# Nine of twelve modulation vectors: from fp32 matmuls and VectorE sums to ScalarE products with GpSimd sums

## Chip, cores and metric

The kernel runs on one core of a Trainium2 chip. The metric is the time of one execution on the device in microseconds (us). Engines are called as the profile calls them: PE (TensorE), ACT (ScalarE), DVE (VectorE), POOL (GpSimd), SP (SyncE, which issues the transfers here).

## What is computed

Two layers of a transformer trunk over 128 context tokens and 128 latent tokens, all in float32, model width D = 2048. Of the reference this matters here:

```
def trunk_layer(x, cond, lp, rope, ctx_k, ctx_v, s0):
    ...
    m = jax.nn.silu(cond) @ w_ada + b_ada
    ...
    sh1, sc1, g1, sh2, sc2, g2 = jnp.split(m, 6, axis=-1)
    h = x * (1.0 + sc1) + sh1
    mix, k, v, s_fin = mixer(h, ...)
    x = layer_norm(DN_ALPHA * x + g1 * mix, ln1_g, ln1_b)
    h = x * (1.0 + sc2) + sh2
    gate, up = jnp.split(h @ w_gate_up, 2, axis=-1)
    ffn = (jax.nn.silu(gate) * up) @ w_down
    x = layer_norm(DN_ALPHA * x + g2 * ffn, ln2_g, ln2_b)
```

The modulation m is one row of 6 x 2048 per stream (context and latent) and layer, made from a 2048 x 12288 matrix w_ada per layer, 201 MB for both. The six vectors of a layer have the numbers 0 to 5 (sh1, sc1, g1, sh2, sc2, g2). The mixer holds the input product (w_in), eight gated DeltaNet heads, attention and the output product (w_o).

## The kernel before

**The large products.** Every weight is read once, 1 MB at a time (`wtile`), into one of two buffers `r`. ACT copies each half as a high part H in fp32r (L382, the "cast"), DVE makes the low part L = r - H (L383). There are three buffers of H and L. PE then multiplies high by high, low by high and high by low: `col_mm` (L413, L414, L417) with the weight as stationary operand, `row_mm` (L390, L391, L393) with the activations as stationary operand. In the feed-forward part of a layer the hidden width is cut in three (HALVES); each third runs w_gate_up tiles, then w_down.

**What runs between.** Both product loops call a hook after every quarter of a tile. In the mixer the hook (`weave`) advances generators of the DeltaNet heads and of attention, and `fill`; in the feed-forward part it is `fill` alone. `fill(n)` adds n to a debt and takes one step of the modulation queue per whole unit, RATES giving n by layer and stage.

**The modulation.** Vectors 0 and 1 of layer 0 are needed first and come from `ada_part`. The other ten stand in `order` and come from `ada_vec`: a vector is 32 tiles of 128 x 1024 of w_ada (one step and one SP load of 512 KB each). On PE a tile is four fp32 matmuls (L253) with the 32 columns of `scT`, which holds silu(cond), as stationary operand; they stand side by side in the array. In the feed-forward part a share of the tiles (DVE_PART) goes to DVE instead: L250 adds tile times scalar to four running sums `side`, the first tile of a run being copied by ACT (L248), and `side_sum` brings them together over the partitions with a matmul of ones (L218). Then the bias is added, and the vector goes to columns (`mods`) or to DRAM (`grow`).

**Who needs a vector when.** `ensure(l, vec)` runs the queue until a vector is done. It stands ahead of the residual with g1, ahead of `fold` for the next layer norm, and ahead of the feed-forward residual with g2; for layer 0 that is right after the first third, since LATE[0] is False. `tail` ends each half of a layer; GAP steps of the queue stand between its two streams.

**The scheduling.** The program hands all this to a scheduler that keeps program order but for priorities (`ahead`, PRI). Each engine then runs its own queue in order. SP issues the weight loads, and each waits for its buffer. POOL has little to do: the memsets, `rsq` (L150, L151), and for each DeltaNet unit an affine_select (L767). L704 and L708 are DVE steps of the DeltaNet heads with two SBUF inputs, L763 one with an input in PSUM.

Of the kernel before, what the change touches and what calls it, by code (L numbers as in the profile page):

```python
# [9 lines left out]
F32 = mybir.dt.float32  # L10
# [25 lines left out]
GAP = (2, 2)  # L36
# [4 lines left out]
LATE = (False, True)  # L41
YLD = (0, 1, 2)
DVE_PART = (0.7, 1.0)
# [3 lines left out]
RATES = ((4.4, 2.0, 1.2), (0.55, 0.6, 0.4))  # L47
# [36 lines left out]
def trunk(ctx: ExitStack, tc: tile.TileContext, A: dict, O: dict):  # L84
# [12 lines left out]
    adap = pool("ada", 1)  # L97
# [6 lines left out]
    def ahead(i):  # L104
        return tc.high_priority(offset=PRI[i]) if PRI[i] else nullcontext()
# [13 lines left out]
    # ------------------------------------------------------------------ constants  # L119
    crow = cp.tile([32, 128], F32, name="crow")  # L120
# [12 lines left out]
    ctan = cp.tile([32, 128], F32, name="ctan")  # L133
# [19 lines left out]
    # ------------------------------------------------------------------ modulation  # L153
# [5 lines left out]
    def ada_part(l, vec, k0, nk, wide=False):  # L159
        """Modulation columns of nk channel tiles (2 or 4) from k0 on."""  # L160
# [20 lines left out]
        br = adap.tile([128, 512], F32, tag="br", name="br")[:, 0:256]  # L181
# [20 lines left out]
    side = {"alloc": None, "ring": None, "part": 0.0, "due": 0.0, "open": None}  # L202

    def side_start(alloc, ring, part):
        side.update(alloc=alloc, ring=ring, part=part, due=0.0)

    def side_stop():
        side.update(alloc=None, ring=None)
        if side["open"] is not None:
            side_sum(False)  # L210

    def side_sum(stop):
        """Add the vector engine's partial products of the open half to the sums of the tensor engine."""
        ps, h, a = side["open"]
        side["open"] = None
        for v in range(2):
            for q in range(4):
                nc.tensor.matmul(ps[32 * q:32 * q + 32, h * 256:(h + 1) * 256], lhsT=ones[:, v, :],  # L218
                                 rhs=a[v][q // 2][:, q % 2 * 256:q % 2 * 256 + 256], start=False,
                                 stop=(stop and v == 1), tile_position=(0, 32 * q))  # L220

    def ada_vec(l, vec):
        ps = psD.tile([128, 512], F32, tag="ada", name="psv")
        started = False
        for h in range(2):
            for kt in range(KT):
                c0 = vec * D + h * 1024
                end = h == 1 and kt == KT - 1
                use = False
                if side["alloc"] is not None:  # L230
                    side["due"] += side["part"]
                    use = side["due"] >= 1.0 and started
                if use and side["ring"] is not None:
                    r = side["ring"]()
                else:
                    r = rawp.tile([128, 1024], F32, tag="a", bufs=RAW[1], name="ra")
                nc.sync.dma_start(r, A["w_ada"][l, kt * 128:(kt + 1) * 128, c0:c0 + 1024])
                if use:
                    side["due"] -= 1.0
                    first = side["open"] is None  # L240
                    if first:
                        side["open"] = (ps, h, side["alloc"]())
                    for v in range(2):
                        for c in range(2):
                            av = side["open"][2][v][c]
                            rc = r[:, c * 512:(c + 1) * 512]
                            if first:
                                nc.scalar.activation(av, rc, AF.Copy, scale=scT[:, kt, v:v + 1])  # L248
                            else:
                                nc.vector.scalar_tensor_tensor(av, rc, scT[:, kt, v:v + 1], av, ALU.mult, ALU.add)  # L250
                else:
                    for q in range(4):
                        nc.tensor.matmul(ps[32 * q:32 * q + 32, h * 256:(h + 1) * 256], lhsT=scT[:, kt, :],  # L253
                                         rhs=r[:, q * 256:(q + 1) * 256], start=not started,
                                         stop=(end and side["open"] is None), tile_position=(0, 32 * q))
                    started = True
                if kt == KT - 1 and side["open"] is not None:
                    side_sum(end)
                if not end:
                    yield  # L260
        br = adap.tile([128, 512], F32, tag="br", name="br")
# [20 lines left out]
    order = [(0, 2), (0, 4), (0, 3), (0, 5)] + [(1, v) for v in (1, 0, 2, 4, 3, 5)]  # L282
# [22 lines left out]
    def ensure(l, vec):  # L305
        while (l, vec) in state["q"] or (state["gen"] is not None and state["cur"] == (l, vec)):
# [6 lines left out]
    # ------------------------------------------------------------------ parameter columns  # L313
# [48 lines left out]
    # ------------------------------------------------------------------ weight tiles and products  # L362
    def wtile(src, nk, n, src2=None, store=None):
# [9 lines left out]
        for j in range(nk // 2):  # L373
# [7 lines left out]
            with ahead(3 if side["alloc"] is None else 4):  # L381
# [42 lines left out]
    class Act:  # L424
        """Transposed activations [channel, channel tile, stream, token] as a high and a low part."""
# [903 lines left out]
```

## Time and profile before

| what | value |
|---|---|
| three runs | 2826.47, 2827.35 (median), 2832.9 us |
| the profiled execution: span from first to last instruction | 2828.9 us; the record has no time outside it |
| instructions | 49217 |
| mean granted PE clock | 0.990 of full speed |
| HBM read / written | 642.88 MB / 8.98 MB, 230 GB/s over the span |

The busy time of an engine is the union of its instructions. An instruction that is held up while it runs counts as busy for all of it. Matmul ends are modelled and overlap, and POOL spans are rough. The idle time in front of a group is put down to what ended it. The stages used below are windows in us from the span's start.

### The profile page before, as it was taken

How to read it: one execution, taken by the hardware profiler on the slowest of the kernel's cores; microseconds unless marked ns; L12 is line 12 of the kernel's file. 1: busy time of each engine (PE TensorE's matmuls, PEld its weight loads, DVE VectorE, ACT ScalarE, POOL GpSimd, SP SyncE). 2: the span in 40 equal slices, each digit the busy share in tenths (PEclk: the TensorE clock that was granted, in tenths of full speed). 3: DMA queues.
4: the chain of work that ended last, by engine and by line, in shares of the span. 5: the costliest groups of instructions: out<-in, count | busy, mean ns of one | idle time of the engine just before them, and what ended most of it. 6: DMA issues, size and time to landing. Idle time of an engine off the chain costs nothing.

```text
span 2828.9 us, 49217 instructions
## 1 busy us (share of the span) xinstructions
PE 2716.8 (96%) x19577; PEld 2321.9 (82%) x19577; DVE 1984.6 (70%) x3008; ACT 1272.6 (45%) x2186; POOL 77.4 (3%) x223
## 2 busy tenths in 40 slices
PE   7999999999999999999999999999899999999998
PEld 5778766667998799878987998877699889998996
DVE  2666877858987878777787587776865855555456
ACT  3324656534444334434435466664444344443442
POOL 0000001000000000000000000100000000000000
PEclk9999999999999999999999999999999999999999
DMA  7888876578888888788876644447766755656555
GB/s 254 262 264 302 260 229 211 175 268 274 271 292 282 299 277 282 262 285 275 277 253 225 227 156 130 156 132 236 254 194 199 250 206 184 211 187 208 184 182 186
DMA packets 406968, 655.08 MB, mean 232 GB/s; under 512 B 19648, under 2 KB 244178, under 8 KB 406610
## 3 DMA queue, kind: packets, MB, share of 16 engines
q1 hardware_dynamic: 406738, 651.94, 70.0%
q8 instruction: 153, 2.51, 0.4%
q14 instruction: 77, 0.63, 0.1%
HBM read 642.88 MB, written 8.98 MB: 230 GB/s over the span
## 4 chain that ended last, share of the span: by engine, by line
PE 47%; DMA 11%; DVE 10%; issue 3%; ACT 3%; POOL 1%; SPq 0%; DVEq 0%; ACTq 0%; POOLq 0%
PE acc L413 10%; PE acc L414 10%; PE acc L417 10%; PE acc L390 4%; PE acc L391 4%; PE acc L393 4%; DMA sa<-w_ada 4%; DVE L L383 4%; DVE side L250 4%; DMA r<-w_down 3%; DMA r<-w_gate_up 3%; ACT H L382 1%; DMA r<-w_o 1%; PE psv L253 1%; PE pr L826 1%
## 5 line engine op out<-in xcount | busy, mean ns | idle before, releaser
L382 ACT ACTIVATE H<-r 128x1024 fp32r<-128x1024 f32 (+1 forms) x770 | 796.1, 1041 | 1202.1 <-PE acc L414 396.0
L383 DVE TENSOR_TENSOR L<-r,H 128x1024 fp32r<-128x1024 f32 (+1 forms) x770 | 922.2, 1201 | 566.5 <-ACT H L382 560.3
L413 PE MATMUL acc<-h2H,H 128*128 128x256 f32 x2816 | 741.6, 285 | 10.3 <-DVE fth L1233 7.8
L414 PE MATMUL acc<-h2L,H 128*128 128x256 f32 x2816 | 736.9, 283 | 0.2 <-DVE h2L L477 0.2
L417 PE MATMUL acc<-h2H,L 128*128 128x256 f32 x2816 | 568.6, 283 | 1.1 <-DVE L L383 0.9
L413 PEld LDWEIGHTS acc<-h2H,H 128*128 128x128 f32 x2816 | 540.6, 192 | 27.4 <-issue 11.9
L414 PEld LDWEIGHTS acc<-h2L,H 128*128 128x128 f32 x2816 | 541.0, 192 | 1.0 <-DVE hf L471 0.4
L417 PEld LDWEIGHTS acc<-h2H,L 128*128 128x128 f32 x2816 | 439.5, 192 | 2.5 <-DVE L L383 2.2
L250 DVE SCALAR_TENSOR_TENSOR side<-sa,scT,side 128x512 f32<-128x512 f32 x480 | 339.1, 745 | 45.4 <-DMA sa<-w_ada 45.0
L390 PE MATMUL acc<-H,dH 128*128 128x512 f32 x672 | 268.9, 400 | 8.7 <-DVE fth L1233 6.0
L391 PE MATMUL acc<-H,dL 128*128 128x512 f32 x672 | 266.2, 396 | 0.0
L413 PE MATMUL acc<-hH,H 128*128 128x256 f32 x768 | 210.1, 295 | 4.3 <-ACT H L382 4.1
L393 PE MATMUL acc<-L,dH 128*128 128x512 f32 x672 | 212.0, 396 | 0.3 <-DVE L L383 0.2
L414 PE MATMUL acc<-hL,H 128*128 128x256 f32 x768 | 203.7, 286 | 0.0
L390 PEld LDWEIGHTS acc<-H,dH 128*128 128x128 f32 x672 | 126.6, 188 | 48.3 <-DVE fth L1233 7.7
L413 PEld LDWEIGHTS acc<-hH,H 128*128 128x128 f32 x768 | 147.8, 192 | 17.7 <-issue 9.1
L417 PE MATMUL acc<-hH,L 128*128 128x256 f32 x768 | 157.7, 288 | 0.1
L390 PE MATMUL acc<-H,hH 128*128 128x392 f32 (+1 forms) x384 | 153.5, 400 | 4.3 <-ACT H L382 4.3
L393 PEld LDWEIGHTS acc<-L,dH 128*128 128x128 f32 x672 | 126.3, 188 | 31.6 <-DVE L L383 1.2
L253 PE MATMUL psv<-ra,scT 128*32 128x256 f32 x1504 | 133.2, 396 | 19.1 <-DMA ra<-w_ada 19.0
L391 PEld LDWEIGHTS acc<-H,dL 128*128 128x128 f32 x672 | 126.6, 188 | 29.4
L414 PEld LDWEIGHTS acc<-hL,H 128*128 128x128 f32 x768 | 148.1, 193 | 1.8 <-issue 1.6
(286 smaller groups left out, 3392.5 us busy)
## 6 DMA issues: line engine op xcount, KB each, us to landing
r<-w_gate_up SPq DMA_DIRECT2D x352, 512.0 KB
ra<-w_ada SPq DMA_DIRECT2D x244, 512.0 KB
r<-w_down SPq DMA_DIRECT2D x88, 1024.0 KB
sa<-w_ada SPq DMA_DIRECT2D x132, 512.0 KB
r<-w_in SPq DMA_DIRECT2D x48, 1024.0 KB
r<-w_o SPq DMA_DIRECT2D x32, 1024.0 KB
r<-w_in SPq DMA_DIRECT2D x24, 784.0 KB
r<-w_in SPq DMA_DIRECT2D x32, 512.0 KB
```

Of the source, the lines that this page charges most:

```text
L250: nc.vector.scalar_tensor_tensor(av, rc, scT[:, kt, v:v + 1], av, ALU.mult, ALU.add)
L253: nc.tensor.matmul(ps[32 * q:32 * q + 32, h * 256:(h + 1) * 256], lhsT=scT[:, kt, :], rhs=r[:, q * 256:(q + 1) * 256], start=not started, ...
L382: nc.scalar.activation(H[:, :w], rs_, AF.Copy)
L383: nc.vector.tensor_tensor(L[:, :w], rs_, H[:, :w], ALU.subtract)
L390: nc.tensor.matmul(a[:, :n], lhsT=act.stat(0, kt, s), rhs=H[:, i, :], start=(first and i == 0), stop=False)
L391: nc.tensor.matmul(a[:, :n], lhsT=act.stat(1, kt, s), rhs=H[:, i, :], start=False, stop=False)
L393: nc.tensor.matmul(a[:, :n], lhsT=act.stat(0, kt, s), rhs=L[:, i, :], start=False, stop=(last and i == 1))
L413: nc.tensor.matmul(a, lhsT=H[:, i, cs], rhs=xH, start=(f and i == 0 and b % 2 == 0), stop=False)
L414: nc.tensor.matmul(a, lhsT=H[:, i, cs], rhs=xL, start=False, stop=False)
L417: nc.tensor.matmul(a, lhsT=L[:, i, cs], rhs=xH, start=False, stop=(la and i == 1 and b % 2 == 1))
L826: nc.tensor.matmul(p[:, d * 128:(d + 1) * 128], lhsT=X[:, d, 0], rhs=v[:, d], start=True, stop=True)
```

## The change

One vector of layer 0, (0, 4), stays with `ada_vec`, now on PE alone. The nine others, (0, 2), (0, 3), (0, 5) and all of layer 1, come from `pool_all`. A vector is four parts of 512 columns. Each step of a part loads two channel tiles (one load of 512 KB), multiplies each by the scalar of each of the two streams on ACT (four 128x512 products, L253 in the new file) and adds them to the two running sums `pacc` on POOL (L256). The products of stream 0 go to a scratch tile `pp` with one buffer, those of stream 1 overwrite the weight tile `pw`, which has two. Three steps into the next part, `pool_finish` sums `pacc` over the partitions with eight matmuls of ones (L264). Steps come from `pfill` in the same hooks, at the rates of POOL_RATES. Besides, LATE[0] becomes True (the gated residual of layer 0 is formed once, in its last third, from rows stored in DRAM), GAP becomes 0, and small buffers move to make room.

```
-GAP = (2, 2)
+GAP = (0, 0)
+PLAG = 3
-LATE = (False, True)
+LATE = (True, True)
-DVE_PART = (0.7, 1.0)
-RATES = ((4.4, 2.0, 1.2), (0.55, 0.6, 0.4))
+RATES = ((1.5, 0.8, 0.0), (0.0, 0.0, 0.0))
+POOL_RATES = ((1.5, 1.5, 0.85), (1.4, 1.4, 0.5))
+POOL_EARLY = 0.5
+PE_ORDER = ((0, 4),)
+POOL_ORDER = ((0, 2), (0, 3), (0, 5), (1, 1), (1, 0), (1, 2), (1, 4), (1, 3), (1, 5))
...
-                if use:
-                    side["due"] -= 1.0
...
-                            if first:
-                                nc.scalar.activation(av, rc, AF.Copy, scale=scT[:, kt, v:v + 1])
-                            else:
-                                nc.vector.scalar_tensor_tensor(av, rc, scT[:, kt, v:v + 1], av, ALU.mult, ALU.add)
...
+    def pool_products(l, vec, part):
+        acc = sidep.tile([128, 2, 512], F32, tag="acc", bufs=2, name="pacc")
+        c0 = vec * D + part * 512
+        for k in range(0, KT, 2):
+            r = sidep.tile([128, 2, 512], F32, tag="w", bufs=2, name="pw")
+            nc.sync.dma_start(r, A["w_ada"][l, k * 128:(k + 2) * 128, c0:c0 + 512].rearrange("(k p) n -> p k n", p=128))
+            pr = sidep.tile([128, 2, 512], F32, tag="p", bufs=1, name="pp")
+            for v, dst in ((0, pr), (1, r)):
+                for i in range(2):
+                    out = acc[:, v, :] if k + i == 0 else dst[:, i, :]
+                    nc.scalar.activation(out, r[:, i, :], AF.Copy, scale=scT[:, k + i, v:v + 1])
+                for i in range(2):
+                    if k + i > 0:
+                        nc.gpsimd.tensor_tensor(acc[:, v, :], acc[:, v, :], dst[:, i, :], ALU.add)
+            yield acc
+
+    def pool_finish(l, vec, part, acc):
+        ps = gps("psf")
+        for v in range(2):
+            for q in range(4):
+                nc.tensor.matmul(ps[32 * q:32 * q + 32, 0:128], lhsT=ones[:, v, :], rhs=acc[:, v, q * 128:(q + 1) * 128],
+                                 start=(v == 0), stop=(v == 1), tile_position=(0, 32 * q))
...
+    def pool_all():
+        last = None
+        for l, vec in POOL_ORDER:
+            for part in range(4):
+                for n, acc in enumerate(pool_products(l, vec, part)):
+                    if n == PLAG and last is not None:
+                        pool_finish(*last)
+                        pdone.add(last[:3])
+                    yield
+                last = (l, vec, part, acc)
...
+    def pfill(n):
+        pdebt[0] += n
+        while pdebt[0] >= 0.5:
+            pdebt[0] -= 0.5
+            next(pool_gen, None)
...
     def ensure(l, vec):
+        if (l, vec) in POOL_ORDER:
+            while (l, vec, 3) not in pdone:
+                next(pool_gen, None)
+            return
...
             def weave(i):
                 fill(RATES[l][i] / 4)
+                pfill(POOL_RATES[l][i] / 4)
...
-                        col_mm(acc, wt, h2, range(4 * g, 4 * g + 4), g == 0, g == 3, lambda: fill(RATES[l][2] / 4, PAIR[0]))
+                        col_mm(acc, wt, h2, range(4 * g, 4 * g + 4), g == 0, g == 3, lambda: pfill(POOL_RATES[l][2] / 4))
...
-    nc = bacc.Bacc("TRN2", target_bir_lowering=False, num_devices=1)
+    nc = bacc.Bacc("TRN2", target_bir_lowering=False, num_devices=1, dynamic_dma_scratch_size=1024)
```

ACT's queue, at the start of the feed-forward part of layer 0, before (H the casts, dH and fth the hidden activations, side and sa the old sums and their tiles):

```order
L1238 ACTIVATE dH<-hx 128x512
L248 ACTIVATE side<-sa,scT 128x512
L382 ACTIVATE H<-r 128x1024 x7
L1232 ACTIVATE fth<-acc 128x512
L382 ACTIVATE H<-r 128x1024 x2
L1238 ACTIVATE dH<-hx 128x512
L382 ACTIVATE H<-r 128x1024 x6
L1232 ACTIVATE fth<-acc 128x512
L382 ACTIVATE H<-r 128x1024
```

The same place after the change:

```order
L412 ACTIVATE H<-r 128x1024
L253 ACTIVATE pp<-pw,scT 128x512
L1265 ACTIVATE dH<-hx 128x512
L412 ACTIVATE H<-r 128x1024
L253 ACTIVATE pp<-pw,scT 128x512
L253 ACTIVATE pw<-pw,scT 128x512 x2
L253 ACTIVATE pp<-pw,scT 128x512 x2
L412 ACTIVATE H<-r 128x1024 x2
L253 ACTIVATE pw<-pw,scT 128x512 x2
```

Where seven casts stood in a row, two now stand between groups of products, which write the tiles that POOL reads.

POOL's queue after the change, in the mixer of layer 0 (X is a DeltaNet matrix, rk the norms of a head):

```order
L256 TENSOR_TENSOR pacc<-pacc,pw 128x512 x2
L797 AFFINE_SELECT X<-X 128x2x128 x2
L256 TENSOR_TENSOR pacc<-pacc,pp 128x512 x2
L154 TENSOR_SCALAR rk<-ss 128x4
L155 TENSOR_TENSOR rk<-rk,mhalf 128x4
L256 TENSOR_TENSOR pacc<-pacc,pw 128x512 x2
```

Before, the affine_selects and the two small steps of rk stood next to each other; now sums stand in front of each and between them.

SP's queue after the change, in w_gate_up of layer 0 (each r tile of weights takes two loads there; y are rows that go to DRAM):

```order
L248 DMA pw<-w_ada 128x2x512
L400 DMA r<-w_gate_up 128x4x256
L248 DMA pw<-w_ada 128x2x512
L401 DMA r<-w_gate_up 128x4x256
L549 DMA xm<-y 128x512
```

The loads of pw stand among those of the large weights, about one and a half to each 1 MB of them.

## Rows read from the trace of the kernel before

**Rows 1.** The page: span, busy time by engine (share, xinstructions); the chain by engine.

```profile
span 2828.9 us, 49217 instructions
PE 2716.8 (96%) x19577; PEld 2321.9 (82%) x19577; DVE 1984.6 (70%) x3008; ACT 1272.6 (45%) x2186; POOL 77.4 (3%) x223
...
PE 47%; DMA 11%; DVE 10%; issue 3%; ACT 3%; POOL 1%; SPq 0%; DVEq 0%; ACTq 0%; POOLq 0%
```

**Rows 2.** The page, costliest groups: xcount | busy us, mean ns | idle before, releaser.

```profile
L250 DVE SCALAR_TENSOR_TENSOR side<-sa,scT,side 128x512 f32<-128x512 f32 x480 | 339.1, 745 | 45.4 <-DMA sa<-w_ada 45.0
...
L253 PE MATMUL psv<-ra,scT 128*32 128x256 f32 x1504 | 133.2, 396 | 19.1 <-DMA ra<-w_ada 19.0
```

**Rows 3.** By stage: us; PE, PEld, DVE, ACT, POOL busy us (xcount); PEclk, DMA share, GB/s.

```profile
108.00:288.00 180.00, 172.74 (x1319) 137.79 (x1318) 116.75 (x210) 62.04 (x83) 2.09 (x6) 1.00 0.84 278
288.00:430.00 142.00, 131.47 (x1207) 94.60 (x1207) 112.86 (x251) 82.10 (x237) 11.04 (x19) 1.00 0.77 249
430.00:637.00 207.00, 200.02 (x1405) 135.99 (x1404) 149.07 (x333) 116.08 (x332) 17.38 (x24) 0.98 0.66 215
637.00:721.00 84.00, 75.84 (x487) 61.48 (x487) 69.91 (x106) 36.24 (x55) 2.34 (x4) 0.94 0.83 269
721.00:1288.00 567.00, 554.28 (x3976) 492.91 (x3976) 457.12 (x566) 224.44 (x241) 1.58 (x3) 1.00 0.85 282
1288.00:2829.00 1541.00, 1496.25 (x10578) 1334.60 (x10576) 1037.04 (x1461) 712.31 (x1168) 38.20 (x103) 0.99 0.62 204
```

**Rows 4.** The same stages, instructions of L383 alone (DVE busy).

```profile
108.00:288.00 180.00, 57.08 (x50) 1.00 0.84 278
288.00:430.00 142.00, 21.59 (x20) 1.00 0.77 249
430.00:637.00 207.00, 36.66 (x30) 0.98 0.66 215
637.00:721.00 84.00, 24.06 (x20) 0.94 0.83 269
721.00:1288.00 567.00, 222.24 (x183) 1.00 0.85 282
```

**Rows 5.** Timeline at 900 us, PE and ACT: start us, us, engine, line, xcount.

```profile
900.84 1.07 PE L218 MATMUL psv<-side,ones 128*32 128x256 f32 x16
...
902.36 2.55 ACT L248 ACTIVATE side<-sa,scT 128x512 f32<-128x512 f32 x4
```

**Rows 6.** POOL by line, three answers: xcount, ns min/median/max, first and last start us.

```profile
L767 POOL TENSOR_SCALAR_AFFINE_SELECT X<-X x32: 406/412/702, 310.7 to 1868.7; 128x256 f32<-128x256 f32 x32
...
L262 POOL MEMSET br<- x10: 524/526/533, 263.2 to 1955.0; 128x512 f32 x10
...
L182 POOL MEMSET br<- x12: 311/312/561, 1.3 to 237.5; 128x256 f32 x12
```

**Rows 7.** Timeline at 1651 us, POOL and DVE instructions.

```profile
1650.86 0.41 POOL L767 TENSOR_SCALAR_AFFINE_SELECT X<-X 128x256 f32<-128x256 f32 x1 [11.28 <-DVE X L763]
1650.91 0.88 DVE L763 SCALAR_TENSOR_TENSOR X<-pe,beta,dk 128x256 f32<-128x256 f32 x2
...
1651.70 0.41 DVE L708 SCALAR_TENSOR_TENSOR vx<-th,cy 128x256 f32<-128x256 f32 x1
...
1651.85 0.53 POOL L767 TENSOR_SCALAR_AFFINE_SELECT X<-X 128x256 f32<-128x256 f32 x1 [0.59 <-DVE X L763]
...
1652.03 1.43 DVE L383 TENSOR_TENSOR L<-r,H 128x1024 fp32r<-128x1024 f32 x1
```

**Rows 8.** Two of the stages, instructions of L704 alone (DVE busy).

```profile
288.00:430.00 142.00, 29.91 (x68) 1.00 0.77 249
430.00:637.00 207.00, 10.90 (x24) 0.98 0.66 215
```

**Rows 9.** Stages, tile psv alone: PE, PEld, DVE busy; last stage and sum.

```profile
1288.00:2829.00 1541.00, 45.02 (x488) 11.97 (x488) 2.72 (x4) 0.99 0.62 204
sum 2829.00, PE 146.77 PEld 38.56 DVE 6.83; mean PE 20.97 PEld 5.51 DVE 0.98
```

More of the change, by code (lines that the diff above doesn't have):

```diff
@@ L96, in trunk @@
     slabp = pool("slab", 6)
-    adap = pool("ada", 1)
+    sidep = pool("side", 1)
     smp = pool("sm", 2)
@@ L180, in ada_part @@
                 yield
-        br = adap.tile([128, 512], F32, tag="br", name="br")[:, 0:256]
+        br = flat(smp.tile([128, 4, 128], F32, tag="hf", name="br"))[:, 0:256]
         nc.gpsimd.memset(br, 0.0)
@@ L201, in trunk @@
         nc.gpsimd.memset(ones[:, v, v:v + 1], 1.0)
[L202 to L220, printed above, removed]
     def ada_vec(l, vec):
         ps = psD.tile([128, 512], F32, tag="ada", name="psv")
-        started = False
         for h in range(2):
@@ L238, in ada_vec @@
-                if use:
-                    side["due"] -= 1.0
-                    first = side["open"] is None
-                    if first:
[L242 to L247, printed above, removed]
-                                nc.scalar.activation(av, rc, AF.Copy, scale=scT[:, kt, v:v + 1])
-                            else:
-                                nc.vector.scalar_tensor_tensor(av, rc, scT[:, kt, v:v + 1], av, ALU.mult, ALU.add)
[L251 to L256, printed above, removed]
@@ L257, in ada_vec @@
-                if kt == KT - 1 and side["open"] is not None:
-                    side_sum(end)
+                r = rawp.tile([128, 1024], F32, tag="a", bufs=RAW[1], name="ra")
+                nc.sync.dma_start(r, A["w_ada"][l, kt * 128:(kt + 1) * 128, c0:c0 + 1024])
+                for q in range(4):
+                    nc.tensor.matmul(ps[32 * q:32 * q + 32, h * 256:(h + 1) * 256], lhsT=scT[:, kt, :],
+                                     rhs=r[:, q * 256:(q + 1) * 256], start=(h == 0 and kt == 0), stop=end,
+                                     tile_position=(0, 32 * q))
@@ new lines, in pool_finish @@
+    def pool_finish(l, vec, part, acc):
+        ps = gps("psf")
+        for v in range(2):
+            for q in range(4):
+                nc.tensor.matmul(ps[32 * q:32 * q + 32, 0:128], lhsT=ones[:, v, :], rhs=acc[:, v, q * 128:(q + 1) * 128],
+                                 start=(v == 0), stop=(v == 1), tile_position=(0, 32 * q))
+        bp = smp.tile([128, 4, 128], F32, tag="hf", name="bp")[:, 0, :]
+        nc.vector.memset(bp, 0.0)
+        c0 = part * 512
+        bsrc = A["b_ada"][l, vec * D + c0:vec * D + c0 + 512].rearrange("(q n) -> q n", q=4)
+        for v in range(2):
+            nc.sync.dma_start(bp[v:128:32, :], bsrc)
+        nc.vector.tensor_tensor(bp, ps[:, 0:128], bp, ALU.add)
+        if vec in (2, 5):
+            for v in range(2):
+                nc.sync.dma_start(grow[l][vec][v, c0:c0 + 512].rearrange("(q n) -> q n", q=4), bp[v:128:32, :])
+        else:
+            pt = gps("pt")
+            nc.tensor.transpose(pt[:, 0:128], bp, ident)
+            nc.vector.tensor_scalar(mods[l][vec][:, part * 4:part * 4 + 4, :],
+                                    pt[:, 0:128].rearrange("p (q x) -> p q x", q=4)[:, :, 0:2],
+                                    1.0 if vec in (1, 4) else 0.0, None, ALU.add)
@@ new lines, in pool_all @@
+    def pool_all():
[8 more added lines that the diff above has]
+                last = (l, vec, part, acc)
+        pool_finish(*last)
+        pdone.add(last[:3])
+    pdone = set()
+    pool_gen = pool_all()
@@ L283, in trunk @@
+    pdebt = [0.0]
+    def pfill(n):
[3 more added lines that the diff above has]
+            next(pool_gen, None)
+    order = list(PE_ORDER)
     state = {"q": list(order), "gen": None, "debt": 0.0}
@@ L380, in wtile @@
                 L = hlp.tile([128, 1024], F32R, tag="L", name="L")
-            with ahead(3 if side["alloc"] is None else 4):
+            with ahead(3 if not ffn[0] else 4):
                 nc.scalar.activation(H[:, :w], rs_, AF.Copy)
@@ L1208, in trunk @@
                 norm.xdst = xm
-            sdp = fx.enter_context(tc.tile_pool(name=f"sd{l}", bufs=1))
-            def side_acc():
-                a = sdp.tile([128, 2, 2, 512], F32, tag="side", name="side")
-                return [[a[:, v, c, :] for c in range(2)] for v in range(2)]
-            side_start(side_acc, lambda: sdp.tile([128, 1024], F32, tag="sa", bufs=2, name="sa"), DVE_PART[l])
+            ffn[0] = True
             stats = smp.tile([128, 2, 4, 6], F32, tag="stats", name="stats")
```

23 lines of the change are left out of this document (9 added, 14 removed).

## The prediction

> **What bounds the kernel now.** Read the page's busy line and chain first [rows 1]: PE is busy for 2716.8 of 2828.9 us, and nearly half of the chain that ended last is PE. So the kernel is one long PE program, and work taken from PE could pay for itself in full. The groups that the change removes come next [rows 2]: 1504 PE instructions of L253, 133.2 us, and 480 DVE instructions of L250, 339.1 us. Then cut the span into stages [rows 3]: 108 to 721 us is the mixer of layer 0, 721 to 1288 most of its feed-forward part, 1288 to the end its remainder and all of layer 1. PE is at 90% or more in each, but ACT is only at 34 to 58% and POOL at 0.3 to 8%. These two look like free room. The question is whether the room is large enough where the change puts the work.
>
> **Where the work goes.** The change makes 36 parts of 16 channel tiles and two vectors: 1152 products on ACT and 1080 sums on POOL (72 products start a sum). The rates are such that all of them are done in layer 0: in the changed ACT order the last product stands before the 324th cast H (L412 there, L382 before). Line up the stages by casts. The five windows hold 50, 20, 30, 20 and 183 of them, counted by L383, which follows each cast [rows 4]. Between the same casts of the changed order stand 170, 136, 120, 111 and 585 products and 158, 128, 112, 105 and 549 sums (30 products and 28 sums lie before 108 us, none behind 1288). A moved unit comes with everything it issues: four products, four sums and one load of 512 KB, 288 loads in all, as many as the tiles they replace, so the bytes stay.
>
> **What a product costs.** The operation exists already: L248 copies a 128x512 tile with a scale per partition, and four in a row take 2.55 us [rows 5], 0.64 us each. With the ACT time there now [rows 3] the five stages need 62.0+108.8 = 171 us of 180, 82.1+87.0 = 169 of 142, 116.1+76.8 = 193 of 207, 36.2+71.0 = 107 of 84, and 224.4+374.4 = 599 of 567 (568 if all 48 old L248 copies fell in this stage). So ACT alone is full in layer 0.
>
> **What a sum costs.** No POOL sum of two 128x512 tiles is in the trace, so it is bounded. A 128x256 affine_select, one read and one write, takes 0.412 us [rows 6]. One that had to let a DVE instruction finish ended 0.27 us behind it (1651.85+0.53 against 1651.70+0.41 [rows 7]); so 0.14 us is start-up, and 512 elements need 0.54 us. Without a second read the sum is 0.14+0.54 = 0.68 us, the low end. The high end is four whole affine_selects, 1.65 us. The memset grows from 0.312 to 0.526 us for 256 more elements [rows 6], 0.43 us per 512 of one stream; a second read stream of that pace gives 0.68+0.43 = **1.11 us**. I take it, because both its parts are POOL rows of this width.
>
> [...]
>
> **What excludes what.** The affine_select at 1651.85 takes 0.53 us instead of 0.412 while an L708 finishes, and the L383 that starts during it takes 1.43 us [rows 7] instead of a mean of 222.2/183 = 1.21 [rows 4]: each is longer by about what the other still had to run. L708 reads two SBUF tiles, as L383 and L704 do. At 1650.86 an affine_select runs beside L763, which reads PSUM, and takes its usual 0.41 [rows 7]. I read this as: a POOL instruction that reads SBUF and a DVE instruction with two SBUF inputs don't run at once.
>
> [...]
>
> So in a stage POOL's sums, POOL's old work [rows 3], L383 [rows 4] and L704 [rows 8] stand one after the other:
> - 108 to 288: 158 x 1.11 + 2.1 + 57.1 = 235 us of 180, +55.
> - 288 to 430: 142.1 + 11.0 + 21.6 + 29.9 = 205 of 142, +63.
> - 430 to 637: 124.3 + 17.4 + 36.7 + 10.9 = 189 of 207, 0.
> - 637 to 721: 116.6 + 2.3 + 24.1 = 143 of 84, +59.
> - 721 to 1288: 609.4 + 1.6 + 222.2 = 833 of 567, +266.
>
> Nothing lets POOL fall behind. A step's scratch tile has one buffer and its weight tile two, so ACT's next products wait for POOL's sums, and behind them on ACT's queue stand the casts that PE waits for, in the mixer also the DeltaNet copies. SP's queue passes it on too: a w_ada load waits until POOL has read the buffer it overwrites, and the weight loads behind it wait with it. On POOL the affine_selects and small powers of the DeltaNet heads now stand between sums. All these are paid within the stage's sum, not on top. PE's clock was granted at 0.94 in the stage where PE idles most, 75.8 of 84 us [rows 3]; I count nothing for it, since PE waits anyway. Together **+443 us**.
>
> **What comes back.** The PE time that L253 frees in layer 0 is hidden there, since PE waits for casts; so are the 36 new groups of eight matmuls, at most 1.07 us each by the old group, which has twice their columns [rows 5]. Behind 1288 us the work is really gone: 45.0 us of psv matmuls [rows 9], in a stage where PE is busy for 1496 of 1541 us [rows 3], so 97% counts: **-44 us**. Nothing I put on three edits. L250's 339 us of DVE were no bound. The late residual of layer 0 needs DVE in a stage with 110 us of DVE idle [rows 3], before L250 leaves. The two steps between the streams at each tail filled PE's wait, which stays as idle time. If that cover is gone, they cost a few us at most.
>
> Sum: 2828.9+443-44 = 3228 us. The median of the runs, 2827.35, is 1.5 us under the profiled span and nothing else lies around it, so the forecast is **3226 us**.
>
> **The rivals.** *First: POOL and DVE don't exclude each other for sums.* For: the affine_select rows are the only witness, and none has two inputs. Against: those rows are clear both ways. Then each stage takes the longer of POOL and ACT: 0, +27 (ACT 169), 0, +35 (POOL 119) and +44 (POOL 611), and -44 behind: 2889 us. The first stage also gets 42 loads of 0.52 MB; on its 278 GB/s, 50 MB, at a DMA share of 0.84 [rows 3] they cost up to 38 us even at a full share: 2927 at most.
>
> *Second, on the other side: POOL and ACT keep up, and PE's relief lands everywhere.* PE loses the psv matmuls, 146.8 us [rows 9]; vector (0, 4) stays with 256 of the 1504 instructions, 22.7 us, and the new sums are at most 38.5: 86 us less, 2742 us. It decides in the feed-forward stage: a sum must take at most (567-1.6-222.2)/549 = 0.63 us with exclusion or 1.03 without, and a product at most 0.64. For it: ACT has slack on both sides of two full stages, and my price of a sum is put together from other operations. Against it: 0.68 is already the price with one read, and four L248 take 2.55 us.
>
> *Third, worse than forecast:* a sum of 1.3 us adds 0.19 x 940 = 179 us in the four full stages, 3405 us. That the change isn't done, or stands elsewhere, is excluded by the instruction order.
>
> **How the numbers follow.** Forecast mechanism 0.66; no exclusion 0.18; POOL and ACT keep up 0.13; beyond 3430 0.03. A measurement of this kernel tells about 0.3% from no change. Faster is the second rival and a corner of the first, 0.14; same is the first rival's lower part, where ACT's slack swallows the waits, 0.05; slower is the rest, 0.81. The range reaches from 2850, a little under the first rival's 2889, to 3430, a little over the costlier sum. It leaves out the second rival, the corner of the first and the far end, 0.2. Within the forecast's own mechanism I expect 3080 to 3430.
>
> **What would show it.** Right: POOL's sums at 1.0 to 1.2 us where no two-input DVE instruction runs, POOL busy for over 65% until its last sum near 1730 us; L413 (the old L383) well over 1.21 us in the mean there; casts in layer 0 that wait behind products, and products that wait for POOL; PE at about 70% in the feed-forward part of layer 0 and at 97% in layer 1. Wrong: sums below 0.7 us, L413 still at 1.21 us while POOL is full, or a layer 0 no longer than now. Then the mechanism falls, whatever the total.

## The result, and the profile after

The changed kernel takes 3507.2 us (median of 4 runs, 3502.99 to 3513.54) against 2828.93 us for the kernel before in the same session: 1.239 times as long, 95% interval 1.236 to 1.242. That is 678 us slower. The forecast was 3226 us, 399 us slower, and the top of its range was 3430 us: the sign was right, the size was not.

The page of the changed kernel: busy lines, the chain that ended last, and four groups (compare [rows 1] and [rows 2]). Line 256 is the sum, 253 the product, 413 the old L383:

```profile
span 3506.6 us, 50267 instructions
PE 2857.5 (81%) x18713; PEld 2464.7 (70%) x18713; DVE 1987.9 (57%) x2583; ACT 1949.0 (56%) x3298; POOL 1672.0 (48%) x1294
PE 39%; POOL 16%; issue 11%; DMA 4%; DVE 4%; ACT 4%; POOLq 0%; SPq 0%; DVEq 0%; ACTq 0%
L413 DVE TENSOR_TENSOR L<-r,H 128x1024 fp32r<-128x1024 f32 (+1 forms) x770 | 1077.6, 1410 | 955.3 <-ACT H L412 932.1
L256 POOL TENSOR_TENSOR pacc<-pacc,pp 128x512 f32<-128x512 f32 x540 | 788.8, 1461 | 284.4 <-ACT pp L253 265.0
L256 POOL TENSOR_TENSOR pacc<-pacc,pw 128x512 f32<-128x512 f32 x540 | 832.7, 1542 | 39.7 <-ACT pw L253 20.3
L253 ACT ACTIVATE pp<-pw,scT 128x512 f32<-128x512 f32 x540 | 364.5, 715 | 392.1 <-DMA pw<-w_ada 327.5
```

POOL went from next to nothing to 1672 us, and all but some 42 us of that lies ahead of 2009 us, in layer 0. The chain now has 16% POOL and only 39% PE. A sum takes 1.50 us in the mean, not 1.11. The next view cuts the span at the same casts as the stages of before [rows 3] (columns: stretch and length, then busy time of PE, PEld, DVE, ACT, POOL, then PE's granted clock, DMA share, GB/s):

```profile
0.00:116.00 116.00, 90.22 (x617) 66.79 (x617) 46.88 (x84) 55.80 (x97) 42.15 (x90) 0.96 0.80 262
116.00:409.00 293.00, 218.66 (x1468) 171.29 (x1468) 157.75 (x242) 171.76 (x266) 236.21 (x166) 0.85 0.74 251
409.00:650.00 241.00, 161.02 (x1121) 114.48 (x1121) 165.07 (x265) 166.44 (x403) 186.62 (x148) 0.83 0.55 177
650.00:902.00 252.00, 183.68 (x1059) 134.46 (x1060) 189.96 (x318) 177.14 (x413) 175.10 (x133) 0.84 0.46 144
902.00:1085.00 183.00, 87.69 (x475) 71.89 (x474) 108.10 (x110) 105.52 (x166) 152.12 (x107) 0.69 0.54 167
1085.00:2009.00 924.00, 667.28 (x3917) 582.53 (x3915) 397.61 (x294) 570.24 (x807) 837.91 (x550) 0.84 0.61 192
2009.00:3507.00 1498.00, 1448.92 (x10061) 1323.23 (x10061) 922.52 (x1272) 702.11 (x1152) 41.84 (x104) 0.98 0.55 176
```

Stage by stage, after less before: 116-108 = +8; 293-180 = +113; 241-142 = +99; 252-207 = +45; 183-84 = +99; 924-567 = +357; 1498-1541 = -43. The four mixer stages together are 969 us instead of 613 (+356), and the sum of all is 678 us. In the feed-forward stage POOL is busy for 838 of 924 us (91%); in the mixer for 750 of 969 (77%). The forecast's own sums had POOL at 75% in the mixer (591 of 790 us), the rest being VectorE instructions that exclude it. Counted from the trace, POOL or a VectorE instruction with two SBUF inputs runs for 857 of the 969 us (88%): no single engine is full there, yet all is late.

What a sum costs, and what it does to VectorE, is seen in the timeline of the feed-forward stage. POOL first, then DVE, the same 12 us; the last line is the group of all 183 L413 of that stage (1.21 us each before [rows 4]):

```profile
1499.51 3.62 POOL L256 TENSOR_TENSOR pacc<-pacc,pw 128x512 f32<-128x512 f32 x2
1503.09 2.65 POOL L256 TENSOR_TENSOR pacc<-pacc,pp 128x512 f32<-128x512 f32 x2
1505.70 3.60 POOL L256 TENSOR_TENSOR pacc<-pacc,pw 128x512 f32<-128x512 f32 x2
1509.26 2.60 POOL L256 TENSOR_TENSOR pacc<-pacc,pp 128x512 f32<-128x512 f32 x2
```

```profile
1499.29 1.34 DVE L413 TENSOR_TENSOR L<-r,H 128x1024 fp32r<-128x1024 f32 x1 [7.38 <-ACT H L412]
1504.59 2.23 DVE L413 TENSOR_TENSOR L<-r,H 128x1024 fp32r<-128x1024 f32 x1 [3.96 <-ACT H L412]
1510.92 2.03 DVE L413 TENSOR_TENSOR L<-r,H 128x1024 fp32r<-128x1024 f32 x1 [4.09 <-ACT H L412]
L413 DVE TENSOR_TENSOR L<-r,H 128x1024 fp32r<-128x1024 f32 x183 | 331.5, 1839 | 384.5 <-ACT H L412 367.4 <-PE acc L423 9.7 <-PE acc L444 5.2
```

Two sums take 2.60 to 2.65 us, also where an L413 starts during the second. A pair that starts during an L413 takes 3.6 us, and an L413 that starts during a sum 2.0 to 2.2 us. Over the trace, 365 sums that met no VectorE instruction took 1.27 us in the mean; from the start of such a sum to the start of the next were 1.29 us (329 pairs).

The same is seen on the mixer's other VectorE lines with two SBUF inputs, and not on those that read PSUM. DVE groups, 116 to 1085 us:

```profile
L413 DVE TENSOR_TENSOR L<-r,H 128x1024 fp32r<-128x1024 f32 (+1 forms) x117 | 178.8, 1544 | 63.6 <-ACT H L412 62.4 <-PE acc L423 0.7 <-ACT v L851 0.4
L734 DVE SCALAR_TENSOR_TENSOR cy<-pad,cv,cy 128x256 f32<-128x256 f32 x96 | 78.6, 839 | 2.0 <-ACT cy L732 1.7
L841 DVE CAST_PREDICATED TP<-lvl,pd 128x512 f16<-128x512 uint8 x80 | 52.3, 683 | 24.9 <-PE pd L837 21.2 <-ACT KQT L767 1.9 <-issue 1.4
L680 DVE TENSOR_TENSOR pad<-acc,pad 128x256 f32<-128x256 f32 x96 | 36.6, 419 | 66.1 <-PE acc L447 66.1
L915 DVE SCALAR_TENSOR_TENSOR ar<-ar,ssa,qkw 128x128 f32<-128x128 f32 x20 | 16.9, 912 | 5.2 <-POOL ssa L155 5.2
L608 DVE SCALAR_TENSOR_TENSOR y<-y,gr 128x512 f32<-128x512 f32 x8 | 11.6, 1473 | 0.0
```

In the mixer of before the same groups had means of 1166, 478, 684, 417, 356 and 688 ns. L841 and L680 read PSUM and are as they were; the other four read two SBUF tiles and take 1.3 to 2.6 times as long.

### The profile page after: what moved, and what is told of

Same layout as the page of the kernel before. It is cut to its first block, busy times and chain, and to the rows that moved or that the text cites. A ratio compares the mean times of both kernels' runs of the same rounds, so it can differ in the third digit from the quotient of the medians.

```text
span 3506.6 us, 50267 instructions
## 1 busy us (share of the span) xinstructions
PE 2857.5 (81%) x18713; PEld 2464.7 (70%) x18713; DVE 1987.9 (57%) x2583; ACT 1949.0 (56%) x3298; POOL 1672.0 (48%) x1294
## 4 chain that ended last, share of the span: by engine, by line
PE 39%; POOL 16%; issue 11%; DMA 4%; DVE 4%; ACT 4%; POOLq 0%; SPq 0%; DVEq 0%; ACTq 0%
POOL pacc L256 15%; PE acc L444 8%; PE acc L443 8%; PE acc L447 8%; PE acc L421 4%; PE acc L420 4%; PE acc L423 4%; DMA pw<-w_ada 2%; ACT pp L253 1%; DVE L L413 1%; DMA r<-w_down 1%; ACT H L412 1%; PE psf L264 0%; DVE y L547 0%; PE pr L856 0%
## 5 line engine op out<-in xcount | busy, mean ns | idle before, releaser
L413 DVE TENSOR_TENSOR L<-r,H 128x1024 fp32r<-128x1024 f32 (+1 forms) x770 | 1077.6, 1410 | 955.3 <-ACT H L412 932.1
L256 POOL TENSOR_TENSOR pacc<-pacc,pp 128x512 f32<-128x512 f32 x540 | 788.8, 1461 | 284.4 <-ACT pp L253 265.0
L443 PE MATMUL acc<-h2H,H 128*128 128x256 f32 x2816 | 787.3, 299 | 128.7 <-ACT H L412 115.5
L256 POOL TENSOR_TENSOR pacc<-pacc,pw 128x512 f32<-128x512 f32 x540 | 832.7, 1542 | 39.7 <-ACT pw L253 20.3
L444 PE MATMUL acc<-h2L,H 128*128 128x256 f32 x2816 | 782.6, 297 | 1.0 <-DVE h2L L507 0.9
L443 PEld LDWEIGHTS acc<-h2H,H 128*128 128x128 f32 x2816 | 580.7, 206 | 141.1 <-ACT H L412 123.4
L447 PE MATMUL acc<-h2H,L 128*128 128x256 f32 x2816 | 600.6, 298 | 38.9 <-DVE L L413 38.1
L444 PEld LDWEIGHTS acc<-h2L,H 128*128 128x128 f32 x2816 | 581.1, 206 | 4.9 <-issue 3.1
L253 ACT ACTIVATE pp<-pw,scT 128x512 f32<-128x512 f32 x540 | 364.5, 715 | 392.1 <-DMA pw<-w_ada 327.5
L253 ACT ACTIVATE pw<-pw,scT 128x512 f32<-128x512 f32 x540 | 361.4, 710 | 0.0
```

The source lines that it names most:

```text
L253: nc.scalar.activation(out, r[:, i, :], AF.Copy, scale=scT[:, k + i, v:v + 1])
L256: nc.gpsimd.tensor_tensor(acc[:, v, :], acc[:, v, :], dst[:, i, :], ALU.add)
L413: nc.vector.tensor_tensor(L[:, :w], rs_, H[:, :w], ALU.subtract)
L443: nc.tensor.matmul(a, lhsT=H[:, i, cs], rhs=xH, start=(f and i == 0 and b % 2 == 0), stop=False)
L444: nc.tensor.matmul(a, lhsT=H[:, i, cs], rhs=xL, start=False, stop=False)
L447: nc.tensor.matmul(a, lhsT=L[:, i, cs], rhs=xH, start=False, stop=(la and i == 1 and b % 2 == 1))
```

## The experiments

Two theories were held against each other at the start. The first: POOL sets the pace of layer 0, at a dearer sum than forecast, and idles where weight tiles or scratch come late. The second: ACT is the engine that is full, since its products stand ahead of the casts that PE waits for. Each experiment was run once, but for the half mix (two runs) and the two small edits (ten); the four runs of the change lie within 11 us of each other, so differences of that size say nothing.

**Without the sums.** Line 255 becomes `if False:`; the sums on GpSimd are left out, so the modulation is not computed.

> Leaves out the 1080 sums on POOL; the 1152 products on ACT, their loads and the matmuls of ones stay. If POOL paces layer 0 (its sums and their exclusion with DVE), the stretch up to the last product shrinks from 2015 us to 1250-1400 and the total is 2790-2900 us. If ACT's products pace it (599 us of ACT in a stage of 567 us), the total stays at 3200 us or more. If the loads of pw pace it, products go on waiting for pw for 300 us or more.

Measured: 2980.09 us, between the first two expectations. Leaving out the sums gives back 527 of the 678 us; 151 stay with the products, their loads and the matmuls of ones. The windows (mixer, feed-forward stage), and two DVE groups of the mixer:

```profile
112.00:854.00 742.00, 603.59 (x4138) 466.17 (x4138) 457.11 (x937) 612.92 (x1244) 29.32 (x50) 0.89 0.75 247
854.00:1490.00 636.00, 576.76 (x3907) 509.39 (x3906) 267.85 (x299) 561.67 (x807) 0.00 (x0) 0.97 0.86 279
```

```profile
L413 DVE TENSOR_TENSOR L<-r,H 128x1024 fp32r<-128x1024 f32 (+1 forms) x118 | 135.3, 1162 | 60.9 <-ACT H L412 60.1 <-PE acc L444 0.8
L734 DVE SCALAR_TENSOR_TENSOR cy<-pad,cv,cy 128x256 f32<-128x256 f32 x96 | 44.2, 486 | 8.8 <-ACT cy L732 8.3
```

VectorE is back at the times of before, so it was the sums that lengthened it. Products alone still cost +129 in the mixer and +69 in the feed-forward stage, with ACT busy for 83 and 88%. The forecast's sums for ACT alone allowed +50 and at most +32.

**The second input of L413 in PSUM.** In layer 0's feed-forward part the subtraction runs in two halves and takes a zero tile in PSUM in place of H (so L is the whole weight there, not its low part).

```diff
-                nc.vector.tensor_tensor(L[:, :w], rs_, H[:, :w], ALU.subtract)
+                    for h0 in range(0, w, 512):
+                        nc.vector.tensor_tensor(L[:, h0:h0 + 512], rs_[:, h0:h0 + 512], zero[0], ALU.subtract)
```

> In the feed-forward part of layer 0, L is made as r minus a zero tile in PSUM, in two halves, so that DVE has one SBUF input there (leaves the subtraction of H out; DVE's time per cast grows from 1.22 to about 1.36 us). Exclusion theory: in the stage of casts 141 to 323 the sums' mean falls from 1.52 to 1.27-1.35 us, DVE's L takes its own time (0.68 us a half), and the stage shrinks from 924 to 780-850 us, the total to 3370-3440. No exclusion: the stage stays at 924 us or grows.

Measured: 3367.04 us, 140 less. The feed-forward stage, and its groups (a half of L is one L416):

```profile
1073.00:1875.00 802.00, 625.46 (x3914) 558.20 (x3912) 297.34 (x479) 571.28 (x808) 704.53 (x550) 0.87 0.70 221
```

```profile
L416 DVE TENSOR_TENSOR L<-r,zero 128x512 fp32r<-128x512 f32 x368 | 231.5, 681 | 401.9 <-DMA r<-w_gate_up 219.7 <-DMA r<-w_down 77.2 <-PE acc L452 62.8
L256 POOL TENSOR_TENSOR pacc<-pacc,pw 128x512 f32<-128x512 f32 x274 | 358.7, 1309 | 14.9 <-ACT pw L253 5.0
L256 POOL TENSOR_TENSOR pacc<-pacc,pp 128x512 f32<-128x512 f32 x276 | 356.8, 1293 | 82.5 <-ACT pp L253 71.8
```

With one SBUF input neither side waits: the sum is 1.30 us (1.55 in that stage of the whole change), a half of L 0.68 us, as L576 of the kernel before, which has one input in PSUM, and the stage is 122 us shorter. So the exclusion is real, and taking it away gives back 122 us in this stage, not the 222 us of whole L383 that the forecast put there.

**Where POOL's idle time comes from.** In the five stages POOL is idle for 1893-1588 = 305 us. The waits name ACT's late products, and behind them the loads:

```profile
ACT pp L253 <- DMA pw<-w_ada: 327.5, 132, 5.4
POOL pacc L256 <- ACT pp L253: 265.0, 91, 28.4
PEld psf L264 <- POOL pacc L256: 160.2, 48, 31.8
```

Five runs each took one link away: the products (all but the 72 that start a sum are left out, by `if k + i == 0:` ahead of line 253, and GpSimd adds the raw weights), the wait at psf (`PLAG = 7`), the two-deep weight tile (`pw` with bufs=3, room from `RAW = (2, 1)`), the loads (288 of them left out, products of a constant tile, no modulation computed), and the single scratch tile (`pp` with bufs=2, same room).

> Leaves out 1080 of the 1152 products: POOL adds the unscaled weights, twice. Sums, loads and exclusion stay. If POOL paces, and its idle time (305 us in the five stages of layer 0) comes from ACT's queue, the total falls by 150-300 us to 3200-3350. If that idle time comes from the pw loads (two buffers, freed by POOL), it stays and the total is 3430-3510. If ACT's products paced layer 0, the total falls below 3000.

> PLAG 7 in place of 3: the eight matmuls of ones stand four steps later in PE's queue, so PE no longer waits for the newest sums there (304 us of waits at psf in the changed kernel). If these waits close a ring PE - ACT - POOL and make POOL's idle time, the total falls by 60-200 us to 3300-3440. If they are only where a wait shows that POOL causes anyway, the total stays within 30 us of 3507 and PE's waits move to casts and L.

> A third buffer for the weight tile of a step, paid with one buffer less for the tiles of the vectors that stay on PE (so the stretch up to 288 us of before may get longer). If POOL's idle time in layer 0 (305 us) is the wait for pw loads whose buffer POOL frees late, the stage of casts 141 to 323 falls from 924 to 840-880 us and products wait for pw for less than half of the 397 us. If the loads wait for something else, the stage stays within 20 us of 924.

> Leaves out the 288 loads of the moved vectors: the products scale a constant tile instead; products, sums, exclusion and the casts stay. If the loads make POOL's idle time (by their latency in a ring of two buffers, or in SP's queue, or by the bytes), POOL is idle for under 120 us in the five stages of layer 0 and the total is 3200-3330 us. If POOL waits for ACT's queue, blocked by casts that wait for PE, the total stays above 3430 us.

> The scratch tile of the products gets a second buffer (room for it from one buffer less for the modulation loads of TensorE). If the single scratch tile couples the two engines, ScalarE can now be a step ahead, and a large part of the 240 us for which GpSimd waits for a product goes: 3300 to 3400 us. If products are late because of what stands before them in ScalarE's queue, a second tile changes little: 3470 to 3515 us, as the third buffer of the weight tile did.

Measured, in that order: 3448.01, 3498.98, 3489.88, 3452.72 and 3509.88 us: -59, -8, -17, -54 and +3, of which -8 and +3 can't be told from nothing. None is the cause alone. The first also settles the second theory: with ACT busy for 316 of 933 us in the mixer and 228 of 902 in the feed-forward stage the time is nearly that of the whole change, so a full ACT is not what paces it. In that run the loads took over: SP's queue stands at the w_ada loads until POOL frees a weight tile, as it does in the whole change (1186.3 us), and the layer's own weights are issued behind them; the casts, with no product ahead of them, wait for those (385.1 us; 41.6 in the whole change). Line numbers are one higher from the sums on:

```profile
SPq L248 <- POOL pacc L257: 1166.9, 256, 12.1
ACT H L413 <- DMA r<-w_gate_up: 385.1, 71, 12.5
```

With three weight tiles, and without loads, the wait for loads only changes its name:

```profile
ACT pp L253 <- POOL pacc L256: 395.4, 176, 5.3
```

```profile
ACT pp L253 <- POOL pacc L256: 506.4, 221, 4.6
```

The first is the third tile, the second the run without loads; in the whole change this wait is 64.3 us. So most of ACT's 327 us of waiting for weights was time in which it would have waited for POOL. With the third tile the feed-forward stage took 903 us, above the 840 to 880 of the first expectation. Without loads the feed-forward stage is 899 us with POOL busy for 854 (95%): there the late products were worth 25 us. In the mixer POOL still idles for 200 of 930 us, so the first expectation of that run (under 120 us in all) falls too.

**Sums alone.** Both the loads and the products but the 72 that start a sum are left out, and GpSimd adds a constant tile (no modulation is computed). It waits for neither.

```diff
-                        nc.gpsimd.tensor_tensor(acc[:, v, :], acc[:, v, :], dst[:, i, :], ALU.add)
+                        nc.gpsimd.tensor_tensor(acc[:, v, :], acc[:, v, :], src, ALU.add)
```

> This kernel leaves out both the 288 weight loads of the parts and all products but the 72 that start a sum; GpSimd adds a constant tile instead, so it waits for neither a transfer nor ScalarE. If GpSimd's idle time in layer 0 (some 305 us in the five stages) comes only from sums whose product is late, the stages shrink to GpSimd's busy time of 1588 us plus some 0.06 us of start-up for each of 1052 sums: 1650 us where they took 1893, 3230 to 3310 us in all, and GpSimd is busy for over 93% of each stage. If GpSimd idles by itself, because its small DeltaNet operations stand in front of the sums and wait for VectorE and ScalarE there, the time stays above 3380 us, with GpSimd idle for 150 us or more in the mixer.

Measured: 3458.77 us: the first expectation fell. The mixer and the feed-forward stage, and the longest waits that involve a sum (every line number is one lower here):

```profile
154.00:1102.00 948.00, 614.83 (x4090) 471.79 (x4089) 632.27 (x933) 318.06 (x737) 776.29 (x560) 0.81 0.37 118
1102.00:1963.00 861.00, 580.21 (x3938) 522.62 (x3938) 400.06 (x301) 238.54 (x256) 805.43 (x510) 0.82 0.36 117
```

```profile
PEld psf L263 <- POOL pacc L255: 323.0, 37, 22.7
ACT pacc L252 <- PE psf L263: 296.9, 27, 21.0
POOL pacc L255 <- ACT pacc L252: 127.8, 11, 27.6
```

The sums alone make layer 0 nearly as long as the whole change does: +46 ahead of the mixer, +335 in the mixer and +294 in the feed-forward stage, where the products alone made +129 and +69, and both together +356 and +357. The prices don't add. With ACT nearly free (34% in the mixer, 28% behind it), POOL still idles for 172 us in the mixer. Its time there is what the second expectation asked for, but the longest waits are not those of DeltaNet's small operations; they point to another ring: PE stops in its queue at psf until POOL has finished a part, ACT's first product of a later part waits for psf to free the accumulator, and POOL waits for that product. That the idle time came only from late products is refuted. That the program's order holds POOL back whatever feeds it is read from the waits; a run of sums alone with a later psf was not made.

**Memsets in place of sums.** As the last run, but each sum is three memsets of 384 elements.

> As the run with sums only, but each of the 1080 sums is three memsets of 384 elements a partition on the same tile (by the memset rows 0.42 us each, 1.26 us in all): GpSimd is held as long as by a sum and reads nothing. The reference's modulation isn't computed. If the price comes from what a sum and VectorE's instructions with two SBUF inputs do to each other, these return to the times of before (L384's group at 1.21 us, the convolution at 0.48 us) and only GpSimd's own pace is left: the feed-forward stage 549 sums of 1.3 to 1.4 us, 700 to 780 us, the mixer 613 to 720 us, 2900 to 3080 us in all. If it is GpSimd's queue (DeltaNet's small operations behind a block of sums, psf behind the last sum), the mixer stays above 850 us and the time above 3200 us.

Measured: 3022.61 us. The windows of the mixer and the feed-forward stage; then a POOL and a DVE group of the feed-forward stage; then VectorE's timeline at 406 us, in the mixer:

```profile
124.00:937.00 813.00, 577.13 (x4088) 447.15 (x4087) 613.34 (x933) 316.06 (x736) 574.44 (x1566) 0.84 0.43 137
937.00:1528.00 591.00, 556.49 (x3936) 506.70 (x3935) 275.56 (x302) 237.47 (x256) 557.24 (x1545) 0.97 0.52 171
```

```profile
L256 POOL MEMSET pacc<- 128x384 f32 x1545 | 557.5, 421 | 21.2 <-ACT pacc L252 21.0
L413 DVE TENSOR_TENSOR L<-r,H 128x1024 fp32r<-128x1024 f32 x183 | 224.0, 1225 | 257.7 <-ACT H L412 257.5
```

```profile
405.88 32.75 DVE L753 TENSOR_SCALAR rkh<-rk 128x2 f32<-128x2 f32 x1 [1.14 <-POOL rk L155]
405.96 32.68 DVE L819 TENSOR_TENSOR TP<-nA,c 128x128 f16<-128x128 f16 x4
```

On POOL, 91 memsets ran meanwhile:

```profile
405.81 32.81 POOL L256 MEMSET pacc<- 128x384 f32 x91
```

The feed-forward stage is clean: 515 triples in 591 us, 1.15 us each (memsets overlap at their edges, so a triple was shorter than meant), L413 at 1.225 us, and the stage 270 us shorter than with sums. Some 70 of these are the shorter hold (1.15 against 1.29 us on 510 sums, an estimate), the rest goes with the reads. So POOL's own pace and the exclusion set that stage; ACT, as nearly free in the run of sums alone, does not. The mixer, 813 us, met neither expectation, and the timeline tells why: a 2-element multiply, L753, takes 32.75 us beside the memsets, and what stands behind it on VectorE ends with it. Six groups of this kind (L753, L199, L538, L489, L978, L971: VectorE instructions with one SBUF input) take 106.7+27.6+23.4+16.0+11.4+6.9 = 192 us in the mixer here, 22 in the whole change and 11 without sums. By an estimate that takes these 170 us away, the mixer would be near 643 us, 30 above before, with POOL busy for 574 us: POOL's queue by itself would then cost little, and most of the 335 us of the sums would come from what their reads do to VectorE. That is worked out, not run, and not all of it is seen: VectorE's busy time in the mixer is 632 us with the sums alone and 457 without sums, 175 more.

**The sums spread out.** `POOL_RATES = ((0.9, 0.9, 0.55), (0.7, 0.7, 0.3))`, `POOL_EARLY = 0.25`, `PLAG = 5`.

> The same work at lower rates, so that products and sums reach to the 520th of 784 casts, into the mixer of layer 1 (PLAG 5). If layer 0 was paced by POOL, a part of its time beyond the casts' own is given back: POOL is no longer full in the feed-forward part of layer 0 and the total is 2980-3200 us. If each product or sum costs a fixed time wherever it stands, the total stays at 3430-3550 us.

Measured: 3299.41 us, 208 less, and still 471 above before, between the two expectations. The feed-forward stage, with 378 sums instead of 548:

```profile
832.00:1555.00 723.00, 594.94 (x3846) 533.43 (x3845) 391.19 (x284) 460.93 (x626) 629.34 (x378) 0.92 0.66 213
```

POOL is busy for 629 of the 723 us (87%), more than any other engine, and by the forecast's own form the stage is 378 x 1.29 + 222 = 710 us. So POOL probably still paces it, though that form counts the exclusion too high. The other 392 sums made what lies behind the stage 1743 us instead of 1541.

**Half the vectors.** Four more vectors go back to fp32 matmuls, so that five are on PE; 600 sums are left, at low rates over both layers (PLAG = 6).

```diff
-PE_ORDER = ((0, 4),)
+PE_ORDER = ((0, 2), (0, 4), (1, 1), (1, 0), (1, 4))
```

> Five of the ten vectors go back to fp32 matmuls; the other five stay on ScalarE and GpSimd, at 0.7, 0.5 and 0.2 of the unit rate in layer 0 and 0.4 and 0.25 in layer 1. 20 parts instead of 36, so some 600 sums, spread over both layers. If a sum costs 1.3 to 1.6 us only where GpSimd has no slack, every stage now has slack (the fullest at some 60% of GpSimd), and the time falls to 2790 to 2950 us. If each sum also takes VectorE's and ScalarE's time in any stage at about the price seen so far (678 us for 1080 sums, 0.63 us each), it is 3150 us or more.

Measured: 3007.33 us, ratio 1.065 (1.057 to 1.074): between the two expectations. The feed-forward stage and the rest, and L413 in the former:

```profile
801.00:1395.00 594.00, 575.55 (x4266) 507.02 (x4255) 330.41 (x275) 305.46 (x373) 237.70 (x142) 0.99 0.81 270
1395.00:3000.00 1605.00, 1493.07 (x10358) 1346.03 (x10356) 1036.72 (x1296) 840.42 (x1389) 401.33 (x326) 0.97 0.58 189
```

```profile
L413 DVE TENSOR_TENSOR L<-r,H 128x1024 fp32r<-128x1024 f32 x183 | 271.5, 1490 | 258.3 <-ACT H L412 253.1 <-PE psv L215 2.8 <-PE acc L423 2.2
```

POOL is 40% busy in that stage and 25% behind it, and the stages are still 27 and 64 us longer than before, the mixer (691 us) 78. Divided by 600 sums, the 185 us between 3007.33 and 2822.71 us (before, in that session) are 0.31 us a sum. Not all of it is the sums': in the feed-forward stage PE is busy for 576 of 594 us (97%), 21 us more than before [rows 3], with 290 more matmuls, since DVE no longer takes a share of the tiles of the vectors on PE. No mix of these rates that was run is as quick as the kernel before.

**The two small edits in the kernel before.** `LATE = (True, True)`, `GAP = (0, 0)`.

> The kernel before with only two small edits of the change: the residual of layer 0 late, and no steps of the queue between the streams of a tail. My working put them at nothing: within 0.3% of before. If the late residual or the empty gaps cost something, 5 to 25 us slower.

Measured: 2828.5 us, ratio 1.000 (0.998 to 1.002). In the kernel before they cost nothing, as forecast.

## Why the prediction was right in its sign and wrong in its size

**The price of a sum failed first.** "A second read stream of that pace gives 0.68+0.43 = 1.11 us": it is 1.27 us alone and 1.29 us from start to start, inside the bounds of 0.68 and 1.65 but above what the rows add up to. In the forecast's split the term that was too small is the second read: its pace was taken from a memset, which only writes, at 0.43 us; from the estimated 0.68 to the measured 1.29 are 0.61. Put into the forecast's five stage sums, 0.18 us more on 158, 128, 112, 105 and 549 sums is +28, +23, +2 (that stage fills up only now), +19 and +99: 171 of the 279 us that were missing. The third rival had 1.3 us and came to 3405 us; it was the nearest, and the forecast left 0.03 for anything beyond 3430.

**"Nothing lets POOL fall behind … All these are paid within the stage's sum, not on top" failed second.** In the mixer the stages with the right price still miss 30, 13, 43 and 21 us, 107 together; POOL is idle there for 219 of 969 us. Part of this is the forecast's list of VectorE instructions that exclude POOL's, L383 and L704 alone, which was too short. VectorE's other lines with two SBUF inputs (L885, L789, L578, L477, L708 and smaller ones) were busy for 5, 9, 32 and 16 us in these stages of before, and they too grew beside the sums (L915 and L608 above are the old L885 and L578). Put in the forecast's way they would be 62 of the 107; that is an estimate, since in the feed-forward stage whole instructions counted too much. VectorE is busy for 621 us in the mixer, 457 without the sums, and L413 and L734, the two lines that the forecast counted, make up 44+34 = 78 of these 164 us. What else the 107 us consist of is not settled: products between the casts, the ring through psf, and PE at a granted clock of 0.82 (651 us busy, against 580 for more matmuls before) are each seen in a trace, but no run took one of them from the mixer alone. A version with sums in the mixer and VectorE's second inputs in PSUM there was not tried.

**The feed-forward stage came out for a mixed reason.** At 1.29 us the form gives 549 x 1.29 + 1.6 + 222 = 932 us, measured 924. But taking the exclusion away gave back 122 us there, not 222; the rest is 95 us by which POOL falls short even without it (802 us for 548 sums, 707 at 1.29). Two errors cancel, which is luck.

**The exclusion was right.** It was read from affine_selects; the run with a PSUM input shows it for sums. What it costs was read too strictly: the affine_select was 0.12 us longer while L708 still had 0.26 to run, and the L383 0.22 longer while the affine_select had 0.35, so about 0.13 us of a meeting overlapped in both rows. The first rival, without exclusion, falls; so does the second, in which POOL and ACT keep up, since it asked for a sum under 0.63 us.

**ACT's price was right, its "full" was not.** The forecast had ACT busy for 171, 169, 193, 107 and 568 to 599 us in the five stages; it was 172, 166, 177, 106 and 570. A product is 0.71 us long, as L248 was, but in a row they overlap:

```profile
1085.00:2009.00 924.00, 375.51 (x585) 0.84 0.61 192
```

These are the products of the feed-forward stage (L253 alone, ACT's busy time), 0.64 us each. What failed is the idea that an engine below 100% costs nothing: without any sum the products and their loads still cost 151 us, with ACT at 83 and 88%. In the whole change most of that is hidden behind POOL, as the run without products shows (-59 us).

**What came back was right**: -44 forecast, -43 measured behind the stage with the last sums, where PE's busy time fell from 1496 to 1449 us. Of the three edits put at nothing, the late residual and the empty gaps cost nothing in the kernel before; that DVE gained nothing by losing L250 was not run by itself. "I count nothing" for PE's clock stands in part: it was granted at 0.69 to 0.85 in the five stages of layer 0 (0.94 and more before [rows 3]), and in the feed-forward stage PE was busy for 667 us at 0.84 where the run without sums had 577 at 0.97 (busy time by clock is 560 us in both), inside a stage that POOL paced.

Of the signs named: POOL was busy for over 65% until its last sum, but that came at about 2009 us, not 1730; L413's mean in layer 0's feed-forward stage was 1.84 us; PE was at 72% there and 97% in layer 1. The sums were above 1.0 to 1.2 us, which was the sign to look at first.

## What to carry to other kernels

Before work goes to an idle engine, price the operation by a measured instruction of the same form and width; where none is there, let the range reach the bound, since here 0.18 us on a thousand instructions were 171 us. A sum on GpSimd, 1.27 us alone, took 1.50 us in the mean here, and L413 beside the sums of the feed-forward stage 1.84 us in place of 1.21: list every VectorE line with two SBUF inputs, not only the largest. And take "the longer of two engines per stage" as a floor only: where products, sums and casts share in-order queues, engines that are 77 to 88% busy already made layer 0 longer.

## What the hardware showed beyond that

Memsets in an unbroken row on POOL held up VectorE instructions with a single SBUF input, which sums did far less: L753, 2 elements a partition, took 13.3 us in the mean and up to 32.75 us in the mixer, against 0.96 us beside sums and 0.17 us without either. L413, with two fp32 SBUF inputs, was at its usual 1.225 us beside the same memsets in the feed-forward stage, and at 1.84 us beside sums. (In the mixer its mean beside memsets is 1.68 us, but 115 of its 120 are at their usual time; the other five stand behind held instructions such as L753.) The wait of L753 at 406 us lasted for a whole row of memsets (91 of them, 32.81 us), not for one of 0.42 us.
